# Where the operands of the key, value and query projections lie in SBUF

## The chip, the cores and the metric

The kernel runs on one core of a Trainium2 chip. The metric is the device time of one execution, in microseconds, as the median of several runs.

## The reference, cut to what matters

The program is one inference step of a small encoder with two layers for 512 frames of a new stream and 64 frames of a running one. The 576 rows are treated together; the model width is 1024 and the inner width of the feed-forward network (FFN) 2816. The first layer mixes by a convolution module, the second by stick-breaking attention; each ends with an FFN. Between them the residual stream is normalised and projected once to keys and values:

```python
def rmsnorm(x, g):
    xf = x.astype(jnp.float32)
    y = xf * lax.rsqrt(jnp.mean(xf * xf, axis=-1, keepdims=True) + EPS)
    return (y * g.astype(jnp.float32)).astype(x.dtype)

def swiglu(xn, w_gu, w_down):
    g, u = jnp.split(xn @ w_gu, 2, axis=-1)
    return (jax.nn.silu(g) * u) @ w_down

for l in range(DEPTH):
    ...
    else:
        if l == N_A_LAYERS:
            k_new, v_new = jnp.split(rmsnorm(h, kv_norm_g) @ w_kv, 2, axis=-1)
        ...
        h = h + sb_attention(rmsnorm(h, b_norm_g[j]), k_all, v_all, q_pos, k_pos, w_q[j], w_o[j])
    h = h + swiglu(rmsnorm(h, ffn_norm_g[l]), ffn_w_gu[l], ffn_w_down[l])
```

## The kernel before

The residual stream h lies transposed in SBUF: eight chunks of 128 channels, each 128 partitions by 576 frames. Every matrix product is made of three matmuls on rounded 32-bit halves: an operand is split into a high part (ScalarE: a copy, or a copy scaled by the norm's gain) and a low part (VectorE: the original less the high part), and TensorE multiplies high by high, high by low and low by high, each in two column halves of 288. Weights are split in the same way as they come in, in pieces of 128 x 512: in the later stages a high part goes to a PSUM bank (hp, L522), another to SBUF (wh, L517), and VectorE subtracts (wl, L527).

The FFN's products use a scheme with seven products in place of eight: blocks of weights and of operands are first added or subtracted on GpSimd (S for weights, ta and tb for operands). An operand pair of that scheme is split by `operands` (L1342 high, L1346 low); `product` (L1431) makes the matmuls of one of the seven products on one of a job's three PSUM banks j_A, j_B, j_C; for the down projection VectorE adds each finished product to h (L1664). The down projection runs in three groups of inner channels (0, 1, 2), each over two runs of two jobs: first the output chunks 0, 4, 1 and 5, then 2, 6, 3 and 7. Behind the last group, each finished chunk is squared (ScalarE, L641 and L635) and the squares are added (GpSimd, L644) for the next norm.

The operands x0 to x7 of the key and value projections are h times a gain, split by `split_x` (L740 high, L744 low). The norm's factor r is applied behind the projection: `Norm.rstd` sums the squares over the channels on TensorE (cs_kv, L726), ScalarE and VectorE make r of it (L682 to L703), and the keys (pk, matmuls at L603, evacuated at L1865) are multiplied by it. The values (vk and pv, L1936) have frames on partitions, so r is turned into a column first: five small matmuls (L1845) into a free corner of the tile vk, copied to rc by VectorE (L1848). Then come the queries (pq, L603), with x split anew under another gain, and the attention.

SBUF places. Sixteen places of 128 x 576 named xh0 to xh7 and xl0 to xl7 (pool `xpool`) belong to x0 to x7: high part of chunk c in xhc, low part in xlc. In the FFNs the same sixteen serve, beside 36 others (f) and two double ones (k), as a common store: `single` takes the place at the front of a list, `give` puts a place at its end once the last product that reads its operand is recorded. In the last run of the down projection, the operands of products 2 and 3 of the four channel pairs lie, among others, in xh3, in xh2 and xh4, in xl0 and xl3, and in xl1 and xh5; product 3 is the last one.

Order of the work. Each operation is recorded with its engine, an estimated cost, and what it reads and writes, its places among them. A planner (class `Plan`) then orders everything between two flushes by these costs and dependencies and writes the instructions out in that order, engine by engine; every engine runs its instructions in order. One flush stands at the end of each FFN, so the splits of x0 to x7 for the keys are planned together with the FFN, and the projections together with the attention.

Of the kernel before, what the change touches and what calls it, by code (L numbers as in the profile page):

```python
# [4 lines left out]
F32R = mybir.dt.float32r  # L5
# [5 lines left out]
P = 128  # L11
D = 1024
NC = D // P
SEQ = 512
DEC = 64
T = SEQ + DEC
# [70 lines left out]
ORDER = (0, 4, 1, 5, 2, 6, 3, 7)  # L87
# [25 lines left out]
class Plan:  # L113
# [19 lines left out]
    def op(self, eng, cost, fn, reads=(), writes=(), lat=0.0, group=None, bias=0.0, urgent=False, port=False):  # L133
        i, deps = len(self.ops), set()
        for k in reads:
            if k in self.w:
                deps.add(self.w[k])
            self.r.setdefault(k, []).append(i)
        for k in writes:
            deps.update(self.r.pop(k, ()))  # L140
            if k in self.w:
                deps.add(self.w[k])
            self.w[k] = i
        deps.discard(i)
        self.ops.append((eng, cost, fn, deps, lat, group, bias, urgent, port or eng == "Pool"))
        self.end.append(0.0)
# [75 lines left out]
def build(tc, xT, vec, st, stp, bdp, wt, ck, cv, w_in, w_out, gu, down, wk, wv, wq, wo, yT, csp, css, kp, ks, vp, vs):  # L222
# [6 lines left out]
    xpool = ctx.enter_context(tc.tile_pool(name="xpool", bufs=1))  # L229
# [81 lines left out]
    h = [h_all[:, c, :] for c in range(NC)]  # L311
    X = {}
# [10 lines left out]
    vecs = base.tile([P, NV], F32, name="vecs")  # L323
# [20 lines left out]
    op = plan.op  # L344
# [15 lines left out]
    def act(n, scaled=True):  # L360
        return 0.186 + n * 0.000834 if scaled else 0.16 + n * 0.000715
# [201 lines left out]
    def by_part(tag):  # L563
        return [(tag, 0), (tag, 1)]
# [7 lines left out]
    def H(m):  # L572
        return [("h", m, 0), ("h", m, 1)]
# [144 lines left out]
    def sums_op(key, tag, parts, halves=(0, 1), segs=None, bias=99.0):  # L718

        for j, (t, dep) in enumerate(parts):  # L720
# [9 lines left out]

            op("PE", 4 * len(halves) * pe(HA), f, reads=[dep], writes=tags(tag), bias=bias)

    def split_x(c, g):


        def hi():
            a, b = (xpool.tile([P, T], F32R, name=f"x{p}{c}_{g}", tag=f"x{p}{c}") for p in "hl")
            X[("xt", c)] = (a, b)
            X[("x", c)] = by_half((a, b))
            nc.scalar.activation(a, h[c], AF.Copy, scale=col(g + c))  # L740

        def lo():
            a, b = X[("xt", c)]
            nc.vector.scalar_tensor_tensor(b, h[c], col(g + c), a.bitcast(F32), op0=ALU.mult, op1=ALU.subtract)  # L744

        op("ACT", act(T), hi, reads=H(c) + ["vecs"], writes=[("x", c, "h")] + by_part(f"xh{c}") + by_part(f"xl{c}"))
        op("DVE", dve(T, True), lo, reads=H(c) + [("x", c, "h")], writes=[("x", c, "l")], port=True)

    xkeys = [("x", c) for c in range(NC)]
# [716 lines left out]
    def ffn(l, mixer, g_next, nrm_next, x_busy, k_busy):  # L1466
# [224 lines left out]
        for g in (1, 2):  # L1691
# [10 lines left out]
                            finished(m)  # L1702
            prepare_operands(force=True)
        if g_next is not None:
            for m in ORDER:
                split_x(m, g_next)
        else:
            tail(l, aops[2], nrm_next, finished)
# [391 lines left out]
    def stages(un):  # L2100
# [135 lines left out]
        def stage_v(pi):  # L2236
# [46 lines left out]
            for (j, a, b, o) in jobs:  # L2283

                def hi(j=j, a=a, b=b, o=o):
                    if ("oh", j) not in X:
                        if j < 6:
                            o2 = tile(("ob", j), f"ob{j}" if j < 4 else f"k{j - 4}", (P, KW), F32R, pool=None if j < 4 else kpool)
                            X[("oh", j)], X[("ol", j)] = o2[:, 0:T], o2[:, T:KW]
                        else:  # L2290
                            X[("oh", j)], X[("ol", j)] = (xpool.tile([P, T], F32R, name=f"o{q}{j}", tag=f"x{q}{j}") for q in "hl")
                        X[("o", j)] = by_half((X[("oh", j)], X[("ol", j)]))
                    nc.vector.tensor_copy(X[("oh", j)][:, a:b], oc[:, o : o + b - a])

                def lo(j=j, a=a, b=b, o=o):
                    nc.gpsimd.tensor_tensor(
                        X[("ol", j)][:, a:b], oc[:, o : o + b - a], X[("oh", j)].bitcast(F32)[:, a:b], op=ALU.subtract
                    )

                fk = ("ok", j)  # L2300
                wk, extra = [fk + (a,)], []
                if fk not in X:
                    X[fk] = True
                    wk += oplace(j) + [fk]
                else:
                    extra = [fk]
                op("DVE", 0.08 + (b - a) / 1920, hi, reads=[("oc", 0), ("oc", 1)] + extra, writes=wk, port=True)
                op("Pool", pool(b - a), lo, reads=[("oc", 0), ("oc", 1)], writes=[fk + (a,)])
# [32 lines left out]
    def oproj(i, m, tag):  # L2341
        wi = take()
        k = ("pw", i, m)
        newps(k, tag)

        def deps(xk):
            j = xk[1]
            own = by_part(f"k{j - 4}") if 3 < j < 6 else by_part(f"xh{j}") + by_part(f"xl{j}") if j > 5 else []
            return [("ok", j, 0), ("ok", j, SEQ)] + oplace(j) + own

        mm_ops(k, tag, wi, [("o", j) for j in range(4 * i, 4 * i + 4)], xdeps=deps)
        add_h(m, k, tag)
# [41 lines left out]
    pp = psum_pool("pp3")  # L2394


    ffn(1, lambda i, m: oproj(1, m, (("b0", "b1"), ("b2", "b3"), ("b4", "b5"))[i % 3]), None, Norm("fin"), XT[12:], KT)
    psum.pop().close()
    ctx.close()

# [92 lines left out]
```

## Time and profile before

| | |
|---|---|
| Time, median of 3 runs | 1216.97 us (1216.84 to 1217.43) |
| Profiled execution | 1216.97 us, span 1215.3 us |
| Granted TensorE clock, mean | 0.997 |
| Busy: TensorE, VectorE, ScalarE, GpSimd | 1189.0, 1017.4, 997.6, 805.1 us |
| Down projection of the first FFN ends, keys begin (TensorE) | 588.24 (start of its last matmul), 589.67 us |
| Column sums of the norm for keys and values (cs_kv) | 596.06 us |
| Queries begin | 621.36 us |

In the profile PE is TensorE, PEld its weight loads, DVE VectorE, ACT ScalarE, POOL GpSimd and SP the engine that issues DMAs. "L1431" is a line of the kernel before. A row of a timeline has the start, the duration, the engine, the line, the instruction with output and inputs, how many instructions it merges, and in brackets the idle time of the engine just before it and what ended that. The listed duration of a matmul reaches past the start of the next, since matmuls are pipelined.

### The profile page before, as it was taken

What the parts mean: (1) busy time and instruction counts of PE and PEld (TensorE: products, weight loads), DVE (VectorE), ACT (ScalarE), POOL (GpSimd) and SP (SyncE); (2) the same over time, 40 slices, a digit from 0 to 9 for tenths busy, and PEclk for the clock granted to TensorE, in tenths of its full rate; (3) what the DMA queues carried; (4) which work ended last, traced back from release to release, by engine and by line L of the source; (5) the groups of instructions that cost most, each with busy time, mean ns of one, the idle gap of its engine ahead of it and who ended that gap; (6) DMA issues with size and microseconds to landing.
All of it is one profiled execution on the core that took longest, in us unless ns stands there. A gap on an engine that the chain in (4) does not pass through costs nothing.

```text
span 1215.3 us, 23815 instructions
## 1 busy us (share of the span) xinstructions
PE 1189.0 (98%) x8670; PEld 1160.6 (95%) x8670; DVE 1017.4 (84%) x1643; ACT 997.6 (82%) x1887; POOL 805.1 (66%) x644
## 2 busy tenths in 40 slices
PE   9999989999999999999999999998999999999996
PEld 9999989999999999999998888998999999999996
DVE  7999977978996766998689999979799966668995
ACT  7998474799888888988669999955998989889983
POOL 1999823497867876996204554464698677789951
PEclk9999999999999999999999999999999999999998
DMA  7233822133133323323364333132232323224222
GB/s 275 85 94 94 267 64 84 53 101 109 53 123 107 102 71 104 105 70 106 121 160 104 74 70 72 48 105 70 70 122 70 122 70 122 88 70 124 86 70 78
DMA packets 44997, 121.07 MB, mean 100 GB/s; under 512 B 8784, under 2 KB 14224, under 8 KB 44880
## 3 DMA queue, kind: packets, MB, share of 16 engines
q1 hardware_dynamic: 44448, 118.98, 32.3%
q8 instruction: 68, 1.11, 0.4%
q10 hardware_dynamic: 432, 0.57, 0.1%
q14 instruction: 49, 0.40, 0.1%
HBM read 105.18 MB, written 5.70 MB: 91 GB/s over the span
## 4 chain that ended last, share of the span: by engine, by line
PE 75%; DVE 10%; POOL 2%; ACT 2%; issue 2%; DMA 1%; SPq 0%; DVEq 0%; POOLq 0%; ACTq 0%
PE j_A L1431 31%; PE j_B L1431 16%; PE j_C L1431 8%; PE po L603 4%; PE pw L603 3%; PE b L2225 3%; PE pq L603 3%; DVE acc L1064 2%; PE b L2132 2%; PE av L2252 1%; DVE wl L527 1%; DMA qd<-qd 1%; PE pk L603 1%; PE pd L603 1%; PE pg L603 1%
## 5 line engine op out<-in xcount | busy, mean ns | idle before, releaser
L517 ACT ACTIVATE wh<-wr 128x512 fp32r<-128x512 f32 (+1 forms) x295 | 179.0, 614 | 35.2 <-PE po L603 15.2
L527 DVE TENSOR_TENSOR wl<-S,hp 128x512 fp32r<-128x512 f32 (+1 forms) x258 | 169.5, 663 | 39.9 <-ACT hp L522 36.8
L527 DVE TENSOR_TENSOR wl<-wr,hp 128x512 fp32r<-128x512 f32 (+1 forms) x233 | 154.2, 666 | 43.2 <-ACT hp L522 38.3
L517 ACT ACTIVATE wh<-S 128x512 fp32r<-128x512 f32 (+1 forms) x260 | 155.8, 610 | 8.1 <-PE j_C L1431 3.1
L522 ACT ACTIVATE hp<-S 128x512 fp32r<-128x512 f32 (+1 forms) x258 | 148.8, 581 | 10.7 <-DVE wl L527 5.0
L522 ACT ACTIVATE hp<-wr 128x512 fp32r<-128x512 f32 (+1 forms) x233 | 134.5, 580 | 19.4 <-DVE wl L527 16.0
L447 POOL TENSOR_TENSOR S<-wr,wr 128x512 f32<-128x512 f32 (+1 forms) x65 | 88.3, 1359 | 84.7 <-ACT wh L517 33.5
L1081 POOL TENSOR_TENSOR pacc<-pacc,pr 128x608 f32<-128x608 f32 x69 | 108.9, 1591 | 7.3 <-ACT pr L1078 4.1
L483 POOL TENSOR_TENSOR S<-wr,S 128x512 f32<-128x512 f32 (+1 forms) x65 | 92.6, 1425 | 26.9 <-DVE wl L527 13.7
L447 POOL TENSOR_TENSOR S<-wr 128x512 f32<-128x512 f32 (+1 forms) x65 | 87.5, 1346 | 21.9 <-ACT wh L517 7.6
L447 POOL TENSOR_TENSOR S<-S,wr 128x512 f32<-128x512 f32 (+1 forms) x65 | 91.2, 1403 | 7.6 <-DVE wl L527 6.7
L1608 POOL TENSOR_TENSOR t<-t,r 128x576 f32<-128x576 f32 x44 | 69.2, 1576 | 4.0 <-ACT t L1579 2.8
L1608 POOL TENSOR_TENSOR a<-a,r 128x576 f32<-128x576 f32 x44 | 70.2, 1599 | 1.0 <-DVE a L1585 0.9
L1064 DVE SCALAR_TENSOR_TENSOR acc<-u,vecs,acc 128x608 f32<-128x608 f32 x76 | 64.6, 850 | 1.0
L1078 ACT ACTIVATE pr<-u,vecs 128x608 f32<-128x608 f32 x69 | 54.1, 796 | 8.0 <-POOL pacc L1081 7.7
L1614 DVE TENSOR_TENSOR a<-a,t 128x576 f32<-128x576 f32 x44 | 51.6, 1173 | 6.3 <-ACT t L1612 5.9
L1579 ACT ACTIVATE t<-j_A 128x288 f32<-128x288 f32 x84 | 34.0, 405 | 22.8 <-PE j_A L1431 21.7
L527 DVE TENSOR_TENSOR wl<-wr,wh 128x512 fp32r<-128x512 f32 x62 | 48.9, 800 | 3.7 <-ACT wh L517 3.7
L2225 PE MATMUL b<-s,sums 128*128 128x512 f32 (+1 forms) x196 | 48.4, 357 | 0.0
L1664 DVE TENSOR_TENSOR h<-j_A,h 128x288 f32<-128x288 f32 x92 | 41.2, 449 | 7.5 <-PE j_A L1431 6.8
L1988 POOL COPY qs<-q 128x64 f32<-128x64 f32 x8 | 3.3, 408 | 54.9 <-DVE q L1985 54.9
L1431 PE MATMUL j_A<-('x', 1, 3)_0_b,wh 128*128 128x288 f32 x168 | 35.9, 295 | 0.0
(987 smaller groups left out, 4535.1 us busy)
## 6 DMA issues: line engine op xcount, KB each, us to landing
wr<-gu SPq DMA_DIRECT2D x88, 512.0 KB, 3.6
wr<-down SPq DMA_DIRECT2D x32, 512.0 KB, 3.8
wr<-w_in SPq DMA_DIRECT2D x15, 512.0 KB, 3.8
wm<-wt SPq DMA_DIRECT2D x12, 576.0 KB, 5.6
wr<-down SPq DMA_DIRECT2D x16, 384.0 KB, 3.1
qd<-qd SPq DMA_DIRECT2D x21, 256.0 KB, 2.9
wr<-w_out SPq DMA_DIRECT2D x8, 512.0 KB, 3.7
wr<-wq SPq DMA_DIRECT2D x8, 512.0 KB, 3.5
```

What stands on the lines that cost most here:

```text
L447: eng(e).tensor_tensor(t[:, :n], x[1](), y[1](), op=ALU.subtract if sub else ALU.add)
L483: eng(e).tensor_tensor(v[:, :n], X[("raw", i0)][:, n : 2 * n], v[:, :n], op=ALU.subtract)
L517: nc.scalar.activation(X[("w", u)][0][:, :n], get(), AF.Copy)
L522: nc.scalar.activation(t[:, :n], get(), AF.Copy)
L527: eng(le).tensor_tensor(b[:, :n], get(), a.bitcast(F32)[:, :n], op=ALU.subtract)
L603: nc.tensor.matmul(o[hf], (hi, hi, lo)[j][:, s], (xh, xl, xh)[j], start=(start and q == 0 and j == 0), stop=(stop and q == n - 1 and j == ...
L1064: nc.vector.scalar_tensor_tensor(dst, src, wt_, dst if i else X[("kneg",)], op0=ALU.mult, op1=ALU.add)
L1078: nc.scalar.activation(tile(("pr", c, i), f"pr{m}", (P, YW)), src, AF.Copy, scale=wt)
L1081: nc.gpsimd.tensor_tensor(X[("pacc", c)], X[("pacc", c)], X[("pr", c, i)], op=ALU.add)
L1431: nc.tensor.matmul(out, a[:, s], b, start=(start and q == 0 and i == 0), stop=(q == len(ops_) - 1 and i == 2), skip_group_check=True,)
L1608: nc.gpsimd.tensor_tensor(X[k], X[k], r, op=ALU.mult)
L2225: nc.tensor.matmul(out(zz()), X[(w,)], get(x), start=False, stop=(i == len(mms) - 1), skip_group_check=True)
```

## The change

A table `xmap` says which two places chunk c takes. It starts as before, (xhc, xlc), and the first projections of the program (convolution module) use it so. At the end of the first FFN it is set anew: the list of free x places stands in the order in which the last operands were given back, and the chunks take places from its front, two each, in the order 0, 4, 1, 5, 2, 6, 3, 7, which is the order in which the rows of h are finished. So x0 lies in xl5 and xl4, x4 in xh0 and xl6, x1 in xl2 and xl7, x5 in xh7 and xh1, x2 in xh6 and xh3, x6 in xh2 and xh4, x3 in xl0 and xl3, and x7 in xl1 and xh5. The places that product 3 of the last run still reads then belong to x2, x6, x3 and x7; before, they belonged to x0, x1, x2, x3, x4 and x5. The queries' operands, two chunks of the attention's output (which take the places of x6 and x7) and the second FFN's list of places that are not free yet follow the same table.

```diff
+    xmap = {c: (f"xh{c}", f"xl{c}") for c in range(NC)}
+
     def split_x(c, g):
 
+        tags_ = xmap[c]
 
         def hi():
-            a, b = (xpool.tile([P, T], F32R, name=f"x{p}{c}_{g}", tag=f"x{p}{c}") for p in "hl")
+            a, b = (xpool.tile([P, T], F32R, name=f"x{p}{c}_{g}", tag=t) for p, t in zip("hl", tags_))
...
-        op("ACT", act(T), hi, reads=H(c) + ["vecs"], writes=[("x", c, "h")] + by_part(f"xh{c}") + by_part(f"xl{c}"))
+        op("ACT", act(T), hi, reads=H(c) + ["vecs"], writes=[("x", c, "h")] + by_part(tags_[0]) + by_part(tags_[1]))
...
         if g_next is not None:
+
+            xmap.update({m: tuple(spots["x"][2 * i : 2 * i + 2]) for i, m in enumerate(ORDER)})
             for m in ORDER:
                 split_x(m, g_next)
...
-                            X[("oh", j)], X[("ol", j)] = (xpool.tile([P, T], F32R, name=f"o{q}{j}", tag=f"x{q}{j}") for q in "hl")
+                            X[("oh", j)], X[("ol", j)] = (xpool.tile([P, T], F32R, name=f"o{q}{j}", tag=t) for q, t in zip("hl", xmap[j]))
...
-            own = by_part(f"k{j - 4}") if 3 < j < 6 else by_part(f"xh{j}") + by_part(f"xl{j}") if j > 5 else []
+            own = by_part(f"k{j - 4}") if 3 < j < 6 else by_part(xmap[j][0]) + by_part(xmap[j][1]) if j > 5 else []
...
-    ffn(1, lambda i, m: oproj(1, m, (("b0", "b1"), ("b2", "b3"), ("b4", "b5"))[i % 3]), None, Norm("fin"), XT[12:], KT)
+    ffn(1, lambda i, m: oproj(1, m, (("b0", "b1"), ("b2", "b3"), ("b4", "b5"))[i % 3]), None, Norm("fin"), [t for t in XT if t in xmap[6] + xmap[7]], KT)
```

The planner writes another order for the end of the first FFN (from about 455 us) and for the key and value projections; from the queries on the order is as before on every engine, but for one DMA issue that stands one row earlier. Lines behind the first insertion have numbers that are larger by 3, later by 5 (L740 is L743, L1664 is L1667, L1845 is L1850). Three places:

ScalarE at the end of the down projection, before (xh4 is the high part of x4, sqn a square of a chunk of h, wh0 the first piece of key weights):

```order
L522 ACTIVATE hp_284_7949<-wr92_7733 128x512
L740 ACTIVATE xh7_72_7955<-h_72,vecs_73 128x576
L517 ACTIVATE wh1284_7947<-wr92_7733 128x512
L522 ACTIVATE hp_283_7972<-wr92_7733 128x512
L522 ACTIVATE hp_286_7980<-wr93_7756 128x512
L517 ACTIVATE wh0283_7970<-wr92_7733 128x512
L740 ACTIVATE xh0_72_7988<-h_72,vecs_73 128x576
L740 ACTIVATE xh4_72_7994<-h_72,vecs_73 128x576
L740 ACTIVATE xh1_72_7998<-h_72,vecs_73 128x576
L740 ACTIVATE xh5_72_8002<-h_72,vecs_73 128x576
L740 ACTIVATE xh2_72_8006<-h_72,vecs_73 128x576
L517 ACTIVATE wh3286_7978<-wr93_7756 128x512
```

and with the change:

```order
L641 ACTIVATE sqn_kv_2_3432_7944<-h_72 128x576
L522 ACTIVATE hp_284_7954<-wr92_7753 128x512
L517 ACTIVATE wh1284_7952<-wr92_7753 128x512
L635 ACTIVATE ss_kv_1_7969<-h_72 128x576
L641 ACTIVATE sqn_kv_6_3434_7975<-h_72 128x576
L522 ACTIVATE hp_283_7982<-wr92_7753 128x512
L522 ACTIVATE hp_286_7993<-wr93_7776 128x512
L517 ACTIVATE wh0283_7980<-wr92_7753 128x512
L743 ACTIVATE xh2_72_7998<-h_72,vecs_73 128x576
L743 ACTIVATE xh6_72_8004<-h_72,vecs_73 128x576
L743 ACTIVATE xh3_72_8008<-h_72,vecs_73 128x576
L522 ACTIVATE hp_285_8014<-wr93_7776 128x512
```

The splits of x0, x4, x1 and x5 have gone from here to earlier rows (x4 to 35 rows ahead of the square of h2 with which the piece begins, x0, x5 and x1 to 6 to 11 rows ahead of it); x2, x6 and x3 follow the first key weights, x7 comes three rows after this piece. The square of h7 (ss_kv_1) stands ahead of the key weights; before, it was the last.

TensorE between keys and values, before (the last key matmuls, the column of r, the first value matmuls):

```order
L603 MATMUL pk_1_0_8062<-xh7_72_7955,wl3286_7979 128x288
L603 MATMUL pk_1_1_8063<-xh7_72_7955,wl3286_7979 128x288
L1845 MATMUL vk_8057<-ident_93,r_97 128x1 x5
L1936 MATMUL vk_8057<-wh0287_8146,xh0_72_7988 128x256
L1936 MATMUL vk_8057<-wh0287_8146,xl0_72_7989 128x256
```

and with the change, 24 value matmuls later:

```order
L1941 MATMUL pv_2_8212<-wh1288_8141,xl3_72_8009 128x256
L1941 MATMUL pv_2_8212<-wl1288_8142,xh3_72_8008 128x256
L1850 MATMUL vk_8059<-ident_93,r_97 128x1 x5
L1941 MATMUL pv_3_8259<-wh0287_8114,xh0_72_7828 128x256
L1941 MATMUL pv_3_8259<-wh0287_8114,xl0_72_7829 128x256
```

The column of r stands behind the first two of the five blocks of value matmuls (vk, pv_2), and a block on another tile (pv_3) follows it.

VectorE in group 1 of the down projection, before ("b1" is the operand of product 1, here of group 2; j_26 is the 26th job):

```order
L1346 TENSOR_TENSOR ('a', 0, 2)_1_b1_6686<-a_0_15_5527,('a', 0, 2)_1_b1_6686 128x288
L527 TENSOR_TENSOR wl4240_6928<-S_26_6_6742,hp_240_6929 128x512
L1664 TENSOR_TENSOR h_72<-j_25_A_6669,h_72 128x288
L1614 TENSOR_TENSOR a_0_21_6482<-a_0_21_6482,t1_0_21_6489 128x576
L1664 TENSOR_TENSOR h_72<-j_25_C_6845,h_72 128x288
L1664 TENSOR_TENSOR h_72<-j_26_C_6912,h_72 128x288
L1346 TENSOR_TENSOR ('a', 0, 2)_2_b1_6698<-a_0_16_5777,('a', 0, 2)_2_b1_6698 128x288
L527 TENSOR_TENSOR wl5241_6972<-S_27_7_6917,hp_241_6973 128x512
L1664 TENSOR_TENSOR h_72<-j_25_A_6669,h_72 128x288
L527 TENSOR_TENSOR wl0242_6984<-S_28_7_6956,hp_242_6985 128x512
L1346 TENSOR_TENSOR ('a', 0, 2)_3_b1_6950<-a_0_17_5844,('a', 0, 2)_3_b1_6950 128x288
L1664 TENSOR_TENSOR h_72<-j_26_A_6755,h_72 128x288
```

and with the change:

```order
L1349 TENSOR_TENSOR ('a', 0, 2)_0_b1_6661<-a_0_14_5459,('a', 0, 2)_0_b1_6661 128x288
L527 TENSOR_TENSOR wl4240_6931<-S_26_6_6750,hp_240_6932 128x512
L1667 TENSOR_TENSOR h_72<-j_25_A_6672,h_72 128x288
L1617 TENSOR_TENSOR a_0_21_6473<-a_0_21_6473,t1_0_21_6489 128x576
L1667 TENSOR_TENSOR h_72<-j_25_C_6847,h_72 128x288
L527 TENSOR_TENSOR wl5241_6968<-S_27_7_6895,hp_241_6969 128x512
L1667 TENSOR_TENSOR h_72<-j_25_A_6672,h_72 128x288
L1667 TENSOR_TENSOR h_72<-j_26_C_6915,h_72 128x288
L1617 TENSOR_TENSOR a_0_20_6452<-a_0_20_6452,t1_0_20_6432 128x576
L527 TENSOR_TENSOR wl1243_6988<-wr80_6790,hp_243_6989 128x512
L1667 TENSOR_TENSOR h_72<-j_26_A_6760,h_72 128x288
```

Of the four product-1 operands of group 2 (pairs 0 to 3), all are split up to here before, and one with the change; the other three follow later.

## The prediction

> **What bounds the kernel now.** I read the page first, then the busy time by stage, then who waited for whom on TensorE around the change, and last the timelines of single engines there.
>
> ```profile
> PE 1189.0 (98%) x8670; PEld 1160.6 (95%) x8670; DVE 1017.4 (84%) x1643; ACT 997.6 (82%) x1887; POOL 805.1 (66%) x644
> PE 75%; DVE 10%; POOL 2%; ACT 2%; issue 2%; DMA 1%; SPq 0%; DVEq 0%; POOLq 0%; ACTq 0%
> ```
>
> TensorE is busy 98% of the span and three quarters of the chain that ended last are its own work. So only time in which TensorE stands still can be won, and anything that makes it stand still is lost. The stages that the change touches are the end of the first FFN's down projection and the key and value projections:
>
> ```profile
> core 0: us, PE busy (x) PEld busy (x) DVE busy (x) ACT busy (x) POOL busy (x), PEclk, DMA share, GB/s
> 500.00:520.00 20.00, 19.63 (x147) 19.19 (x146) 19.70 (x32) 17.87 (x33) 18.11 (x14) 1.00 0.33 106
> 520.00:540.00 20.00, 19.47 (x147) 19.24 (x146) 19.13 (x33) 17.98 (x34) 20.00 (x17) 1.00 0.34 106
> 540.00:560.00 20.00, 20.00 (x151) 19.83 (x150) 19.38 (x33) 16.05 (x30) 13.31 (x12) 1.00 0.31 85
> 560.00:580.00 20.00, 20.00 (x153) 20.00 (x152) 14.53 (x28) 18.12 (x33) 12.31 (x10) 1.00 0.32 102
> 580.00:600.00 20.00, 18.54 (x131) 17.58 (x130) 13.62 (x22) 14.61 (x26) 6.24 (x8) 1.00 0.35 116
> ```
>
> The columns that matter are PE, DVE, ACT and POOL busy out of 20 us. The granted clock is 1.00 throughout. From 500 to 560 DVE has hardly a gap (19.70, 19.13, 19.38); from 560 on DVE and ACT have room. TensorE's largest loss is in the last stretch. Its waits from 400 to 640 us, by cause (total, times, longest):
>
> ```profile
> PE pk L603 <- ACT xh L740: 1.1, 1, 1.1
> PE j_A L1431 <- DVE h L1664: 0.8, 2, 0.5
> PE pk L603 <- DVE xl L744: 0.3, 1, 0.3
> PE vk L1936 <- DVE rc L1848: 0.3, 1, 0.3
> ```
>
> They sum to 2.5 us, so nothing here can be worth many microseconds. The list counts only idle time; a matmul's listed end reaches past the start of its successor, so I take the loss from the distance of starts. The first row below is a piece of the chain of waits (start, duration, matmuls), the others are TensorE's timeline (start, duration, instruction, count, idle time before it and what ended it):
>
> ```profile
> 598.16 7.18 PE pk L603 x54
> 588.24 0.29 PE L1431 MATMUL j_A<-('a', 0, 2)_3_b,wl 128*128 128x288 f32 x1
> 589.67 0.53 PE L603 MATMUL pk<-xh,wh 128*128 128x288 f32 x2 [1.14 <-ACT xh L740]
> 590.53 0.53 PE L603 MATMUL pk<-xl,wh 128*128 128x288 f32 x2 [0.32 <-DVE xl L744]
> 596.06 2.10 PE L726 MATMUL cs_kv_None<-ss_kv,ones 128*128 128x288 f32 x8
> ```
>
> Undisturbed, 54 matmuls of 288 columns take 7.18 us, 0.133 each. The last matmul of the down projection starts at 588.24, so the first key matmul (pk) could start at 588.37. It starts at 589.67, when the high part of x0 is there (1.30 lost), and the low part of x0 holds the third matmul until 590.53, against 589.94 (0.59 lost). Up to the norm's column sums (cs_kv) at 596.06 stand 42 key matmuls: 42 x 0.133 = 5.59, which from 588.37 ends at 593.96. **Lost at this boundary: 596.06 - 593.96 = 2.10 us.**
>
> **The change, part by part.** It adds and removes no instruction. Each operand chunk x0 to x7 gets two places in SBUF, and only the assignment changes; the order written by the planner follows from it.
>
> (1) *The boundary.* Before, places held to the last product belong to six of the eight chunks, x0 to x5; now they belong to x2, x3, x6 and x7, whose h rows are finished last anyway. The splits of x0, x4, x1 and x5 go ahead of the last three products. What is the last wait now? The timeline of ScalarE, and last a row of VectorE's:
>
> ```profile
> 582.71 0.69 ACT L641 ACTIVATE sqn_kv<-h 128x576 f32<-128x576 f32 x1 [2.93 <-DVE h L1664]
> 585.00 0.69 ACT L641 ACTIVATE sqn_kv<-h 128x576 f32<-128x576 f32 x1 [0.57 <-POOL ss_kv L644]
> 585.59 0.58 ACT L522 ACTIVATE hp<-wr 128x512 fp32r<-128x512 f32 x1
> 588.34 0.61 ACT L517 ACTIVATE wh<-wr 128x512 fp32r<-128x512 f32 x1
> 588.86 3.43 ACT L740 ACTIVATE xh<-h,vecs 128x576 fp32r<-128x576 f32 x5
> 589.66 3.73 DVE L744 SCALAR_TENSOR_TENSOR xl<-h,vecs,xh 128x576 fp32r<-128x576 f32 x5
> ```
>
> Start to start, a square (sqn) takes 0.59, a bank copy (hp) and a weight split (wh) 0.52 each, an x split 0.67 (3.43 for five); five low parts on VectorE take 3.73, 0.75 each. The key projection needs wh of its first weights, which ended at 588.95 before, and it now becomes the late one. The square of h2 opens the row. It started at 582.71, on h2's last update. In the new order the last three matmuls of that product stand behind the next product of twelve, so it comes 12 x 0.133 = 1.6 us later, at 584.3. Behind it stand in the new order square, hp, wh, square, square, hp, hp and then the wh: 3 x 0.59 + 4 x 0.52 = 3.85, so the wh starts at 588.15, with 0.05 more for Pool's addition in front of the third square (a wait that was 0.57), and ends at 588.8. TensorE starts at 588.9 instead of 589.67, and its first 24 matmuls (x0, x4, x1, x5; 3.2 us) find both parts ready. Then x2, x6, x3 follow the wh on ScalarE from 588.7; x7 comes after them, one hp and two wh: 588.7 + 3 x 0.67 + 3 x 0.52 = 592.3, its low part by 593.9. TensorE wants it 42 matmuls after 588.9, at 594.5: 0.6 to spare. The column sums now follow 54 key matmuls, at 588.9 + 7.18 = 596.1, and need the last square (593.0 to 593.7) and Pool's addition:
>
> ```profile
> 593.99 1.43 POOL L644 TENSOR_TENSOR ss_kv<-ss_kv,sqn_kv 128x576 f32<-128x576 f32 x1 [4.71 <-ACT sqn_kv L641]
> ```
>
> 593.7 + 0.1 + 1.43 = 595.2, so 0.9 to spare. Loss at the boundary now: 588.9 - 588.37 = 0.53. **Gain 2.10 - 0.53 = 1.57.** Bounds: 0.59 if the wh only ends when x0 did before (589.6), 2.10 if h2's square is not late.
>
> (2) *The column of r for the values.* TensorE waits there for a copy on VectorE (two rows of TensorE's timeline, one of VectorE's, two pieces of the chain of waits):
>
> ```profile
> 607.61 0.28 PE L1936 MATMUL vk<-wl,xh 128*128 128x256 f32 x1
> 608.15 0.39 PE L1936 MATMUL vk<-wh,xh 128*128 128x256 f32 x1 [0.26 <-DVE rc L1848]
> 607.93 0.17 DVE L1848 COPY rc<-vk 128x5 f32<-128x5 f32 x1 [2.26 <-PE vk L1936]
> 609.84 4.32 PE pv L1936 x36
> 621.36 12.00 PE pq L603 x90
> ```
>
> Value matmuls go at 4.32 / 36 = 0.12. After 607.61 the next could start at 607.73; it starts at 608.15: 0.42 lost. The copy waited 2.26 us, until the twelve value matmuls on the same PSUM tile (vk) had passed, though what it reads was written before them. In the new order these twelve and twelve more stand ahead of the r columns, and twelve on another tile behind them (1.44 us), so the copy is done under those. **Gain 0.42**, bounds 0 (the copy is late behind the k rows, which VectorE now takes first) and 0.42. r itself comes later, since the new order puts two weight splits ahead of its last step on VectorE (2 x 0.68 by a row below), but 24 x 0.12 = 2.9 us of value matmuls now stand ahead of its reader. From here the value matmuls and the first queries (pq) run without a gap in the chain, and the order after them is unchanged on every engine, so I take the gain to reach the end whole.
>
> (3) *The down projection itself.* The planner also wrote another order back to about 455 us. What it can win is bounded by TensorE's two large stalls there, and what it can lose by VectorE (rows of both timelines):
>
> ```profile
> 506.81 0.29 PE L1431 MATMUL j_B<-('a', 0, 1)_3_b,wl 128*128 128x288 f32 x1
> 507.41 0.51 PE L1431 MATMUL j_A<-('a', 0, 1)_0_b,wh 128*128 128x288 f32 x2 [0.31 <-DVE h L1664]
> 520.39 0.29 PE L1431 MATMUL j_B<-('a', 0, 1)_3_b,wl 128*128 128x288 f32 x1
> 521.22 0.54 PE L1431 MATMUL j_A<-('a', 0, 1)_0_b,wh 128*128 128x288 f32 x2 [0.53 <-DVE h L1664]
> 501.71 0.45 DVE L1346 TENSOR_TENSOR ('a', 0, 2)_0_b<-a,('a', 0, 2)_0_b 128x288 fp32r<-128x288 f32 x1
> 512.70 1.26 DVE L1346 TENSOR_TENSOR ('a', 0, 2)_1_b<-a,('a', 0, 2)_1_b 128x288 fp32r<-128x288 f32 x1
> 516.85 1.58 DVE L1346 TENSOR_TENSOR ('a', 0, 2)_2_b<-a,('a', 0, 2)_2_b 128x288 fp32r<-128x288 f32 x1
> 518.36 0.68 DVE L527 TENSOR_TENSOR wl<-S,hp 128x512 fp32r<-128x512 f32 x1
> 519.91 0.88 DVE L1346 TENSOR_TENSOR ('a', 0, 2)_3_b<-a,('a', 0, 2)_3_b 128x288 fp32r<-128x288 f32 x1
> ```
>
> 507.41 - 506.81 - 0.133 = 0.47 and 521.22 - 520.39 - 0.133 = 0.70: 1.17 in all, both released by an update of h on VectorE, which came late behind operand and weight splits. In the new order three of the four group-2 low halves shown (1.26, 1.58, 0.88) and three weight splits (0.68) fewer stand ahead of the twelfth h update. That work is not gone: it lies behind, between 520 and 560. Upper bound 1.17; lower bound below. **I take half, 0.6.** The extra ScalarE work before 588 costs nothing: four x splits, 4 x 0.67 = 2.7 us, where ScalarE idled 2.93 us in one piece (row 582.71). On SP one load of query weights moves up by one row; nothing waits for it there.
>
> Sum: 1.57 + 0.42 + 0.6 = 2.6 us. The profiled execution took 1216.97 us (1.67 around its span), the same as the median shown, so I forecast **1214.4 us**.
>
> **Rivals.**
>
> *A: the weights take the place of the operands.* If ScalarE reaches the wh of the first weights only when x0 was ready before, TensorE starts at 589.67 as it did, and only x0's low part (0.59) and the column copy (0.42) are won: 1216.97 - 1.0 = 1216.0. For it: ScalarE does everything in order, and in front of this wh stand three squares, each with a wait (h2, h7, Pool). Against it: the walk above has 0.8 us left.
>
> *B: everything goes.* h2's square is not late, the wh is early, and both stalls of the down projection vanish: 2.10 + 0.42 + 1.17 = 3.7, so 1213.3. For it: at the second stall the new order puts another product of nine matmuls (1.2 us) in front of the one that waited.
>
> *C: slower; VectorE falls behind from 520 to 560.* There it idles 0.87 + 0.62 = 1.49 us. The work moved in is 1.26 + 1.58 + 0.88 + 3 x 0.68 = 5.76 by the rows. If TensorE has to wait for all that does not fit, it loses 4.27, less the 1.99 of (1) and (2): 1216.97 + 2.3 = 1219.3. It decides from the point where the overflow exceeds 2 us. For it: POOL is busy 20.00 of 20 us from 520 to 540, and the same low half took 0.45 us in one place and 1.58 in another. The Trainium skill, page "SBUF — State Buffer", section "Who interferes with whom", says that a VectorE instruction with two SBUF inputs contends with a GpSimd instruction that reads SBUF; these low halves are such instructions, and the trace agrees (0.45 against 1.58). By that rule the moved halves stay long in the new place. Against it: VectorE idles over 5 us from 560 to 580, so an overflow drains there unless a product needs it sooner.
>
> *D: no effect.* The splits stay where h lets them be; 1217.0. The changed order speaks against it.
>
> **How the numbers follow.** Forecast 0.45, A 0.26, B 0.22, C 0.05, D 0.02. A measurement of this kernel tells about 0.2% (2.43 us, below 1214.54) from no change. B and a little more than half of the forecast's spread (0.28) lie beyond it: faster 0.50. A, D and the rest of the forecast's (0.17) lie within: same 0.45. Slower 0.05. The range runs from a little below B, 1212.8, to a little above A, 1216.6; the forecast's own is 1213.6 to 1215.2.
>
> **What would show it.** In the changed profile: the first key matmul starts within 0.7 us of the down projection's last, with a ScalarE weight split and no x split as its releaser, and no wait for a low part follows; the wait for the column copy is gone; the stretch from 500 to 540 shows less than the 0.84 us of TensorE idle that two of its waits have now, and 540 to 560 none over 0.3. Wrong would be: a wait of the key matmuls for x2 or x7, of the column sums for Pool, or of down products for group-2 operands of more than 1 us; or an x split that still stands as releaser of the first key matmul.

## The result and the profile after

The changed kernel takes 1219.70 us (median of 14 runs, 1218.6 to 1220.34); the kernel before took 1217.23 on the same chip (14 runs). The ratio is 1.0019, 95% interval 1.0012 to 1.0026: **2.5 us slower**, where 2.6 us less was forecast. The profiled execution took 1219.54 us, its span is 1217.8.

Up to the attention's last product the change does what was forecast. TensorE's waits from 400 to 640 us and its timeline at the boundary, and a row of ScalarE's timeline:

```profile
PE j_A L1434 <- DVE h L1667: 0.7, 2, 0.4
PE pk L603 <- ACT wh L517: 0.4, 1, 0.4
```

```profile
588.19 0.29 PE L1434 MATMUL j_A<-('a', 0, 2)_3_b,wl 128*128 128x288 f32 x1
588.86 0.55 PE L603 MATMUL pk<-xh,wh 128*128 128x288 f32 x2 [0.37 <-ACT wh L517]
596.17 2.11 PE L726 MATMUL cs_kv_None<-ss_kv,ones 128*128 128x288 f32 x8
588.19 0.61 ACT L517 ACTIVATE wh<-wr 128x512 fp32r<-128x512 f32 x1
```

The first key matmul starts 0.67 us behind the last down product (before: 1.43) and waits for a weight split, no x split. No wait for a low part or for the column of r is left. The 54 key matmuls end with the column sums at 596.17, so 588.19 + 0.133 + 7.18 = 595.50 leaves 0.67 lost (before: 2.10). What makes the kernel slower stands 200 us later. TensorE at the end of the attention, before, and then with the change (av is the attention's output, ob, oh and ol operands of the output projection, pw its products):

```profile
795.00 0.78 PE L2252 MATMUL av<-e,vv 128*128 128x512 f32 x2
795.62 0.99 PE L603 MATMUL pw<-ob,wh 128*128 128x288 f32 x4
800.85 0.53 PE L603 MATMUL pw<-oh,wh 128*128 128x288 f32 x2
802.57 0.54 PE L603 MATMUL pw<-ol,wh 128*128 128x288 f32 x2 [1.19 <-POOL ol L2296]
```

```profile
793.00 0.63 PE L2257 MATMUL av<-e,vv 128*128 128x512 f32 x2
798.31 0.85 PE L603 MATMUL pw<-ob,wh 128*128 128x288 f32 x4 [4.69 <-DVE oc L2283]
799.44 1.16 PE L603 MATMUL pw<-ob,wh 128*128 128x288 f32 x4
802.30 0.69 PE L603 MATMUL pw<-ob,wh 128*128 128x288 f32 x4
```

The last attention product starts at 793.00 instead of 795.00: 2.00 won so far. Two matmuls of 0.24 later the output projection of the second half of the heads could begin, at 793.48. It begins at 798.31: **4.83 us lost in one wait**, for the row oc on VectorE, the last step of copying av out of PSUM (its evacuation). Before, the same product began at 795.62, 0.14 after it could. Behind the wait the matmuls are slow: 18 of them take 3.99 us from 798.31 to 802.30 instead of 18 x 0.133 = 2.39, another **1.60**. In return the waits of 0.30 (at 795.62 to 796.45, before) and 1.46 (800.85 to 802.57) are gone, since those operands are ready by now. -2.00 + 4.83 - 0.14 + 1.60 - 1.76 = +2.53 at this place; the spans differ by 2.5.

What the wait hangs on (one row each of GpSimd, ScalarE and VectorE), and the stretches by granted clock (TensorE's busy time in 2 us, PEclk):

```profile
794.70 0.76 POOL L2301 TENSOR_TENSOR ol<-oc,oh 128x64 fp32r<-128x64 f32 x1
795.49 1.20 ACT L2280 ACTIVATE oc<-av 64x512 f32<-64x512 f32 x2 [1.93 <-POOL ol L2301]
796.77 1.39 DVE L2283 TENSOR_TENSOR oc<-av,oc 64x512 f32<-64x512 f32 x2 [1.49 <-issue]
```

```profile
core 0: us, PE busy (x), PEclk, DMA share, GB/s
794.00:796.00 2.00, 0.00 (x0) 1.00 0.47 131
798.00:800.00 2.00, 1.69 (x9) 0.71 0.09 30
800.00:802.00 2.00, 2.00 (x10) 0.50 0.84 225
802.00:804.00 2.00, 2.00 (x16) 0.93 0.09 37
```

ScalarE's copy of av (oc) waits for GpSimd, which still reads the tile oc of the pair before; VectorE's addition follows, ends at 798.16, and 0.15 later TensorE goes on. The granted clock then stands at 0.71 and 0.50 and comes back by 804.

**Why the same product did not wait before.** The order on TensorE is the same there; what it waits for is not. The program's own rows, before and with the change:

```
4804 L603 MATMUL pw_4_0_10573<-ob_10031,wh_10350 128x288 [waits DVE_49]
4805 L603 MATMUL pw_4_1_10574<-ob_10031,wh_10350 128x288 [waits DVE_49]

4804 L603 MATMUL pw_4_0_10573<-ob_10031,wh_10350 128x288 [waits DVE_49,PE_49,Activation_49]
4805 L603 MATMUL pw_4_1_10574<-ob_10031,wh_10350 128x288
```

The reason is the PSUM bank. A PSUM pool of this kernel gives a tag its banks when the first tile of that tag is made, and the tile is made where the planner puts the matmul that opens it (`newps`, an operation without cost). The re-planned order makes the column sums of the norm (cs_kv) before the tiles of values and keys. From the addresses in the two programs:

| banks | before | with the change | next pool, in both |
|---|---|---|---|
| 0, 1 | vk, last used as av | cs_kv, last used as scores b4, b5 | cs_f |
| 2, 3 | pk_0, last used as pw_7 | vk, last used as **av** | **pw_4**, the first product |
| 4, 5 | cs_kv, last used as b4, b5 | pk_0, last used as pw_7 | pw_0 |
| 6, 7 | pk_1, last used as b2, b3 | pk_1, last used as b2, b3 | pw_1 |

The next pool opens at the end of the attention. Its first product lies in banks 2 and 3 in both kernels; before, these held pw_7, which VectorE had read, and now they hold av, the last thing that the attention leaves.

### The profile page after: what moved, and what is told of

The parts are those of the page before. It is cut to its first block, busy times and chain, and to the rows that moved or that the text cites. A ratio compares the mean times of both kernels' runs of the same rounds, so it can differ in the third digit from the quotient of the medians.

```text
span 1217.8 us, 23814 instructions
## 1 busy us (share of the span) xinstructions
PE 1189.6 (98%) x8670; PEld 1161.7 (95%) x8670; DVE 1021.1 (84%) x1643; ACT 997.7 (82%) x1887; POOL 808.6 (66%) x644
## 4 chain that ended last, share of the span: by engine, by line
PE 74%; DVE 9%; ACT 2%; issue 2%; DMA 2%; POOL 1%; SPq 0%; DVEq 0%; POOLq 0%; ACTq 0%
PE j_A L1434 30%; PE j_B L1434 15%; PE j_C L1434 7%; PE po L603 4%; PE pw L603 4%; PE b L2230 3%; PE pq L603 3%; PE b L2137 2%; DVE wl L527 1%; DVE acc L1067 1%; PE av L2257 1%; DMA qd<-qd 1%; PE pk L603 1%; PE pd L603 1%; PE pg L603 1%
## 5 line engine op out<-in xcount | busy, mean ns | idle before, releaser
L1667 DVE TENSOR_TENSOR h<-j_A,h 128x288 f32<-128x288 f32 x92 | 41.4, 450 | 4.4 <-PE j_A L1434 3.8
L603 PE MATMUL pw<-ob,wh 128*128 128x288 f32 x192 | 34.5, 303 | 4.7 <-DVE oc L2283 4.7
```

The lines of the kernel that those rows point to most:

```text
L603: nc.tensor.matmul(o[hf], (hi, hi, lo)[j][:, s], (xh, xl, xh)[j], start=(start and q == 0 and j == 0), stop=(stop and q == n - 1 and j == ...
```

## The experiments

Starts on TensorE in the profiles (us), and medians. Each ratio is against runs of the kernel before on the same chip, whose median was 1217.44 us beside e1 to e4, 1217.65 beside e5 to e8 and 1217.63 beside e9 and e10:

| kernel | last down product | first key matmul | first product pw_4 | first gate matmul | median | ratio, interval |
|---|---|---|---|---|---|---|
| before | 588.24 | 589.67 | 795.62 | 824.91 | 1217.23 | |
| change | 588.19 | 588.86 | 798.31 | 827.20 | 1219.70 | 1.0019 (1.0012, 1.0026) |
| e1 banks of before | 586.52 | 587.19 | 792.08 | 821.37 | 1214.24 | 0.9975 (0.9965, 0.9984) |
| e2 banks of change | 586.78 | 588.21 | 798.95 | 828.91 | 1222.10 | 1.0037 (1.0024, 1.0049) |
| e3 matmuls in the wait | 586.61 | 587.28 | 796.28 | 823.59 | 1216.11 | 0.9992 (0.9983, 1.0001) |
| e4 own oc | 586.47 | 587.13 | 792.04 | 820.08 | 1212.59 | 0.9962 (0.9949, 0.9974) |
| e5 change again | 586.70 | 587.36 | 797.00 | 826.23 | 1219.84 | 1.0018 (1.0009, 1.0027) |
| e6 before again | 588.30 | 589.73 | 795.86 | 825.14 | 1217.29 | one run |
| e7 light VectorE | 586.45 | 586.85 | 791.79 | 821.08 | 1213.70 | 0.9972 (0.9960, 0.9983) |
| e8 places reversed | 588.31 | 590.39 | 797.17 | 826.45 | 1218.63 | 1.0006 (0.9997, 1.0014) |
| e9 best banks, own oc | 586.98 | 587.64 | 792.50 | 820.39 | 1212.93 | 0.9962 (0.9948, 0.9975) |
| e10 change, own oc | 586.39 | 587.06 | 795.13 | 823.91 | 1217.25 | 0.9996 (0.9987, 1.0004) |

### Order and banks, one at a time (e1, e2)

To the changed kernel e1 adds tiles that are made once, in a fixed order, right after the pool is opened:

```diff
     pp = psum_pool("pp2")
+    for i, (tag, n) in enumerate([('v', 2), ('b0', 1), ('b1', 1), ('b4', 1), ('b5', 1), ('b2', 1), ('b3', 1)]):
+        tile(("first", i), tag, (P, 512 * n), pool=pp)
```

> The changed kernel with one addition: right after the PSUM pool of the attention part is opened, its tiles are created once in the order of the kernel before (v, b0, b1, b4, b5, b2, b3), so that each name gets the PSUM banks that it has in the kernel before. The order of instructions on every engine is that of the changed kernel. Theory P (the loss is the PSUM banks: the re-planned order created the column sums' tiles first, so the first output product of the second FFN's section inherits the banks of the attention's last tile av): the 4.83 us wait at 793 us goes, the slow matmuls behind it too, the small waits of the kernel before come back (0.30 and 1.46), and the gain up to 640 us stays: 1217.2 - 2.0 = 1215.2. Rival S (the loss is the SBUF places: the attention's outputs o6 and o7 or the second FFN's free places moved with the table): the wait stays, 1219.7. Rival N (any re-planning moves the end by some us either way): no prediction, but 1215.2 within 0.3 would be a coincidence.

To the kernel before, e2 adds the same lines with the order b4, b5, v, b0, b1, b2, b3.

> The kernel before, whose order stays, with the tiles of the same pool created once in the order of the changed kernel (b4, b5, v, b0, b1, b2, b3). Theory P: the same wait appears at about 795 us without any change of the operands' places: 4.83 us of wait and 1.6 us of slower matmuls behind it, less the 0.30 and 1.46 that the kernel before loses there: 1217.2 + 4.5 = 1221.7. Rival S: 1217.2, no wait there.

Both leave the order of every engine as it was; only waits of a few matmuls differ. TensorE's timelines, e1 and then e2:

```profile
791.46 0.78 PE L2259 MATMUL av<-e,vv 128*128 128x512 f32 x2
792.08 0.99 PE L603 MATMUL pw<-ob,wh 128*128 128x288 f32 x4
797.30 0.53 PE L603 MATMUL pw<-oh,wh 128*128 128x288 f32 x2
799.02 0.53 PE L603 MATMUL pw<-ol,wh 128*128 128x288 f32 x2 [1.18 <-POOL ol L2303]
```

```profile
793.51 0.78 PE L2254 MATMUL av<-e,vv 128*128 128x512 f32 x2
798.95 1.30 PE L603 MATMUL pw<-ob,wh 128*128 128x288 f32 x4 [4.66 <-DVE oc L2280]
```

With the banks of before the wait is gone, and e1 takes 1214.24: 3.2 us less than the kernel before and 5.5 less than the changed one. With the banks of the change, the kernel before gets the wait (4.96 lost, with no edit to places or order) and takes 1222.1, 4.7 us more. Theory P said 1215.2 and 1221.7. S (places in SBUF) is out, and so is N (any re-planning), since nothing is re-planned in e2 and the wait is there. e1 is a microsecond better than P said; its profile reaches the last down product 1.67 earlier than the first one of the change (more on that below).

### What the wait is made of (e10, e3)

e10 is the changed kernel, banks included, in which the last pair's oc lies in a place of x0 that is free by then:

```diff
+            own = {0: oc}
+            if un.i == len(pairs) - 1:
+                own.clear()
+            def place_oc():
+                if not own:
+                    own[0] = xpool.tile([P, T], F32, name="oc2", tag=xmap[0][0])
+                return own[0]
...
-                    return two(oc[m, :w])
+                    return two(place_oc()[m, :w])
```

(the two operations behind it read `place_oc()` likewise).

> The changed kernel with its own banks, and the own place for the last pair's oc as in e4_own_oc: nothing but the evacuation of av gets earlier. Theory P (the first output product waits until VectorE has read av): ScalarE's copy of av need not wait for GpSimd, VectorE's addition then starts behind its two weight splits, 1.5 us earlier, and the wait of 4.83 us falls to about 3.4; 1219.7 - 1.5 = 1218.2 if the clock still falls to one half behind it, 1216.6 if it does not. Rival W (it waits for the weights, which ScalarE splits behind the copy): the wait stays over 4.5, 1219.5.

Rows of TensorE, ScalarE and VectorE in e10:

```profile
791.27 0.78 PE L2257 MATMUL av<-e,vv 128*128 128x512 f32 x2
795.13 1.30 PE L603 MATMUL pw<-ob,wh 128*128 128x288 f32 x4 [3.09 <-DVE oc L2290]
792.08 1.20 ACT L2287 ACTIVATE oc<-av 64x512 f32<-64x512 f32 x2 [0.25 <-PE av L2257]
793.61 1.38 DVE L2290 TENSOR_TENSOR oc<-av,oc 64x512 f32<-64x512 f32 x2
```

The copy now follows av by 0.25 us, VectorE's addition ends at 794.99, and TensorE goes on at 795.13: lost 795.13 - 791.27 - 0.48 = 3.38, as said. The wait is the evacuation of av. The clock falls again, so of the two cases it is that of 1218.2; the median of 1217.25 is 0.95 better. The span is 2.2 us shorter than e5's: 1.6 is the wait, and about 0.45 the slow clock behind it (28.78 against 29.23 us from the first product to the first gate matmul).

e3 lets TensorE work through the wait of the changed kernel:

```diff
     flush()
+    hold = pp.tile([P, 512], F32, name="hold", tag="b2")
+    for i in range(18):
+        nc.tensor.matmul(hold, X[("oner",)], vv[0], start=True, stop=True)
     section()
     att_pool.close()
```

> The changed kernel with 18 matmuls of 512 columns on a free PSUM bank behind the last attention product, so that TensorE works through most of the 4.83 us wait (18 x 0.24 = 4.3 us) and nothing else moves. Theory C (part of the loss is that TensorE runs slower after a long wait: the granted clock is 0.97 and 0.94 in the two stretches around it, and the 18 matmuls after it take 1.6 us more than 18 x 0.133): the wait's end stays where it is, the matmuls behind it run at 0.133 each, 1219.7 - 1.6 = 1218.1, and the granted clock stays 1.00. Rival L (they are slow because weights or operands come late): 1219.7, still slow.

TensorE's timeline and its clock by stretches in e3, then the clock in e5, the changed kernel once more:

```profile
792.17 4.27 PE L2399 MATMUL hold<-vv,sums 128*128 128x512 f32 x18
796.28 0.69 PE L603 MATMUL pw<-ob,wh 128*128 128x288 f32 x4
```

```profile
796.00:798.00 2.00, 2.00 (x16) 1.00 0.04 9
```

```profile
796.00:798.00 2.00, 1.00 (x4) 0.50 0.40 145
798.00:800.00 2.00, 2.00 (x10) 0.50 0.48 76
800.00:802.00 2.00, 2.00 (x13) 0.71 0.49 195
```

With work in it the clock stays at 1.00 and four matmuls take 0.53 us again; in e5 the clock is at 0.50 from 796 to 800, while four matmuls take 0.96 (798.58 to 799.54). From the first product to the first gate matmul the changed kernel takes 28.89 and 29.23 us in its two profiles, e3 27.31: the slow clock costs 1.6 and 1.9, where theory C of e3 said 1.6. e3 is faster than the 1218.1 of this theory. In its profile the time from the last attention product on is shorter too (796.28 - 791.56 - 0.48 = 4.24 us against 4.96 in e5): the edit also moved two squares on ScalarE behind the added matmuls, GpSimd reached the last read of oc earlier, and VectorE had finished by 795.1. That part was not meant.

### The places themselves (e8)

On top of e1, the table is turned round:

```diff
-            xmap.update({m: tuple(spots["x"][2 * i : 2 * i + 2]) for i, m in enumerate(ORDER)})
+            xmap.update({m: tuple(spots["x"][14 - 2 * i : 16 - 2 * i]) for i, m in enumerate(ORDER)})
```

> As e1_banks_of_before, with the table of places turned round: the places that are held to the last product go to x0, x4, x1 and x5, which the key projection wants first, and the free ones to the others. Theory (first term of the prediction: what counts is that the first chunks' places are free before the last product): the splits of x0 stand behind the last down product again, the first key matmul comes about 1.3 us behind it and the low part holds the third by 0.6, so the boundary loses about 2.1 as in the kernel before, instead of 0.54: e1_banks_of_before + 1.5 = 1215.7, and 0.4 more if the column of r waits again. Rival N (any re-planning with the same banks does it): 1214.2.

TensorE's timeline at the boundary, and a stretch by clock:

```profile
588.31 0.29 PE L1434 MATMUL j_A<-('a', 0, 2)_3_b,wl 128*128 128x288 f32 x1
590.39 0.53 PE L603 MATMUL pk<-xh,wh 128*128 128x288 f32 x2 [1.78 <-ACT xh L743]
591.24 0.62 PE L603 MATMUL pk<-xl,wh 128*128 128x288 f32 x2 [0.32 <-DVE xl L747]
592.14 0.68 PE L603 MATMUL pk<-xh,wh 128*128 128x288 f32 x2
```

```profile
592.00:594.00 2.00, 2.00 (x10) 0.50 0.98 398
```

The two waits are back, for the x split and its low part, 1.95 and 0.59 us, and here they too halve the clock: from 591.66 to 594.54 twelve matmuls take 2.88 us instead of 1.60. 1218.63 is 4.4 us above e1 (5.0 by the spans), where 1.5 was expected. N is out: with the same banks, which chunk gets which places decides between a gain of 3.2 us and none. The size was missed by the clock (1.3), a first wait longer by 0.65 than in the kernel before, and 1.8 us in the down projection of this profile. The last need not be chance: the planner's order for the reversed table is close to that of the kernel before (in the two programs, 63 of TensorE's matmuls stand elsewhere than there, 420 elsewhere than in the change), and the stalls of the kernel before are back with it (0.42 at 519 us, 0.69 at 521).

### The down projection (e5, e6, e7)

e5 and e6 are the changed kernel and the one before, unchanged, for second profiles. e7 is e1 with each update of h in the first FFN's down projection on 32 columns instead of 288, so it leaves out most of what this projection adds to h.

> The changed kernel once more, unchanged, for a second profile on the chip of the next three. Question: its first profile has three stalls of TensorE in the down projection (0.52, 0.53 and 0.24 us, released by updates of h on VectorE) and reaches the last down product at 588.19; the runs with the banks of before, whose order is the same there, have none of them and reach it at 586.52. Theory J (VectorE has no slack from 500 to 560, and whether its stalls reach TensorE falls out anew in each execution): the profile shows either picture, and the times lie in groups about 1.5 us apart. Rival B (the bank placement itself acts back on the down projection): the three stalls are there again, and 588.2.

> The kernel before once more, for a second profile. First profile: stalls of 0.47 and 0.70 and smaller ones, last down product at 588.24; the run with the banks of the change and the order of before has one of 0.47 and reaches it at 586.78. Theory J: either picture, times in groups about 1.5 us apart (1216 and 1217.4). Rival B: 588.2 again.

> As e1_banks_of_before, and each update of h in the first FFN's down projection takes 32 columns instead of 288 (most of what that down projection adds is left out), at the same place of VectorE's order and at the same planned cost, so that the order of all engines stays. That takes some 0.27 us off each of the about 45 updates from 500 to 560, so VectorE has over 10 us of slack there. Theory J (the third term of the prediction is VectorE's slack): no stall over 0.2 us from 455 to 586, the last down product at 586.5 or a little before, and the times in one group near the faster one of e1_banks_of_before, 1213.8 within 0.4. Rival D (the spread of the times comes from the transfers of the first 200 us or from the end): the times of e1_banks_of_before with both groups, median 1214.2.

Rows of TensorE in the first profile of the change, in its second, and in the second of the kernel before:

```profile
537.57 0.51 PE L1434 MATMUL j_A<-('a', 0, 1)_0_b,wh 128*128 128x288 f32 x2 [0.35 <-DVE h L1667]
546.54 0.50 PE L1434 MATMUL j_A<-('a', 0, 2)_0_b,wh 128*128 128x288 f32 x2 [0.37 <-DVE h L1667]
```

```profile
586.70 0.29 PE L1434 MATMUL j_A<-('a', 0, 2)_3_b,wl 128*128 128x288 f32 x1
```

```profile
521.28 0.53 PE L1431 MATMUL j_A<-('a', 0, 1)_0_b,wh 128*128 128x288 f32 x2 [0.53 <-DVE h L1664]
588.30 0.29 PE L1431 MATMUL j_A<-('a', 0, 2)_3_b,wl 128*128 128x288 f32 x1
```

In its first profile the change has traded the stalls at 507 and 521 for others at 537, 546 and 566 (0.52, 0.53, 0.24). In its second they are all but gone, and the last down product comes at 586.70, as in e1, e3, e4, e9 and e10, which have the same order up to there. The order before reaches it at 588.24, 588.30 and, in e2, 586.78. So rival B is out, and **the same program reaches this product some 1.5 us earlier or later from execution to execution**: late in one of seven profiles of the new order, in two of three of the old, which is too few to speak of odds. A part of it comes before this stage. The last matmul up to which both orders agree starts at 444.38 and 444.83 in the two profiles of the kernel before, and at 444.77 and 444.49 in those of the change. From there to the last down product it takes 143.86 and 143.47 before, 143.42 and 142.21 with the change. In e7 no stall of over 0.2 us is left there, the last product comes at 586.45, and 4 of 6 runs take 1213.5 to 1213.7; two are at 1214.7 and 1215.5, so VectorE's slack is not all of the spread; what the rest is stays open. The busy time of the engines there, change and e7 (the third figure behind 20.00 is VectorE's, 20.00 and 14.74):

```profile
540.00:560.00 20.00, 19.63 (x148) 19.42 (x147) 20.00 (x35) 15.95 (x29) 9.77 (x8) 1.00 0.29 84
540.00:560.00 20.00, 20.00 (x153) 20.00 (x153) 14.74 (x32) 15.94 (x30) 11.06 (x10) 1.00 0.32 107
```

### Beyond the change (e4, e9)

e4 is e1 with the own place for oc of e10.

> As e1_banks_of_before, and the last pair's output column tile oc lies in a place of x0, which is free by then, so that ScalarE's copy of av need not wait until GpSimd has read the tile of the pair before (idle 2.08 us before it in the kernel before, released by the low part on GpSimd). Theory: the copy starts about 2 us earlier, VectorE's addition 1.5 us earlier, the low part of the last output operand ends at about 800.8 on the clock of the kernel before instead of 802.5, and TensorE's 1.46 us loss there goes: 1215.2 - 1.4 = 1213.8. Rival: another wait is right behind it (the weights of the next product, ScalarE's weight splits) and half or more comes back: 1214.5 to 1215.2.

In e4 the wait of 1.46 for the last low part is down to 0.33:

```profile
797.73 0.54 PE L603 MATMUL pw<-ol,wh 128*128 128x288 f32 x2 [0.17 <-POOL ol L2310]
```

1212.59 us, 4.9 less than the kernel before; where 1.4 less than e1 was expected, 1.65 came. e9 gives the first product the banks that are free earliest:

> As e4_own_oc (the changed kernel with the banks given by hand, and an own place for the last pair's oc), but the banks are given in the order v, b4, b5, b0, b1, b2, b3: the first output product of the second FFN's section gets the banks of the attention's scores (b4, b5), which are free earliest, and the second one those of the product before (b0, b1). Theory P: the 0.30 us that TensorE loses at the first output product in e4_own_oc goes, nothing else moves: 1212.6 - 0.3 = 1212.3. Rival: the low part of the last output operand is waited for by 0.3 more: 1212.6.

```profile
792.50 0.69 PE L603 MATMUL pw<-ob,wh 128*128 128x288 f32 x4
798.20 0.53 PE L603 MATMUL pw<-ol,wh 128*128 128x288 f32 x2 [0.47 <-POOL ol L2310]
```

The loss of 0.30 behind the first product is gone, and the wait for the low part has grown from 0.33 to 0.64: the rival was right, 1212.93 is not better. What bounds here is the chain from av to that low part.

## Why the prediction was wrong, point by point

**The step that failed** is the last sentence of part (2): the order behind the values is unchanged on every engine, "so I take the gain to reach the end whole". An unchanged order does not mean unchanged waits. The new order ahead of it made the tiles of the attention's pool in another sequence, so the banks changed, and the first product behind the attention inherited av's. e1 and e2 show it from both sides: by the medians the banks alone cost 4.7 us on the old order and 5.5 on the new. No rival had this. C came closest in number (1219.3) by a mechanism that did not occur.

**What bounds the kernel**: right. What moved in these profiles was TensorE's waits and its clock behind them, not its work; but what was read as "nothing here can be worth many microseconds" holds for a gain from waits that are there, and says nothing of a wait that is not there yet.

**(1) The boundary**: right. First key matmul forecast at 588.9, measured 588.86, its releaser the weight split; no wait for x2 or x7; column sums forecast at 596.1, measured 596.17. Gain forecast 1.57, measured 2.10 - 0.67 = 1.43. e8 shows that it hangs on the order of the places.

**(2) The column of r**: right. 0.42 was forecast, 0.49 came: from the column sums to the first query matmul it takes 25.14 us before (596.06 to 621.20; the 621.36 given ahead is a row of the chain of waits) and 23.05 with the change (596.17 to 619.22). 1.60 of the 2.09 are the twelve key matmuls that now stand ahead of the sums. VectorE's copy no longer holds TensorE:

```profile
607.79 0.16 DVE L1853 COPY rc<-vk 128x5 f32<-128x5 f32 x1 [0.74 <-PE vk L1850]
```

**(3) The down projection**: right in kind, wrong as one number. 0.6 was half of the stalls of one profile. From 444 us on the stage takes 143.4 to 143.9 us or 141.8 to 142.5 in these profiles; in the first pair the change gains 0.44 there, in the second 1.26. That it makes the short time more frequent is not shown by so few. By the medians e1 wins 3.2, so (1) and (2) leave about 1.3 for it, a little over the upper bound of 1.17.

**The sum**: with the banks held, 1214.24 was measured where 1214.4 was forecast. That they lie so close is in part luck: 3.2 us were won where 2.6 were forecast, and the kernel before took 1217.44 beside e1, not the 1216.97 that the forecast started from.

**Rival C** priced the three moved low halves at the durations they had, and took from the rule on contention (the Trainium skill, "SBUF — State Buffer", "Who interferes with whom") that they would stay long. In the new place they took half of that:

```profile
521.27 0.57 DVE L1349 TENSOR_TENSOR ('a', 0, 2)_1_b<-a,('a', 0, 2)_1_b 128x288 fp32r<-128x288 f32 x1
537.71 0.80 DVE L1349 TENSOR_TENSOR ('a', 0, 2)_2_b<-a,('a', 0, 2)_2_b 128x288 fp32r<-128x288 f32 x1
542.43 0.55 DVE L1349 TENSOR_TENSOR ('a', 0, 2)_3_b<-a,('a', 0, 2)_3_b 128x288 fp32r<-128x288 f32 x1
```

0.57, 0.80 and 0.55 instead of 1.26, 1.58 and 0.88. What differs is how much was left of the instruction that GpSimd was running when the low half began. Two rows of GpSimd, the one under the low half of 1.58 before and the one under that of 0.57 with the change:

```profile
516.82 1.30 POOL L447 TENSOR_TENSOR S<-S,wr 128x512 f32<-128x512 f32 x1
520.71 0.81 POOL L1377 TENSOR_TENSOR ('a', 0, 2)_0_tb<-a,('a', 0, 2)_0_tb 128x288 f32<-128x288 f32 x1
```

The first ends at 518.12 and its low half at 518.43, the second at 521.52 and its low half at 521.84; all six end 0.31 to 0.33 us behind such an instruction. So they do contend with GpSimd, as that rule has it; that a moved one stays long does not follow.

**A, B, D**: A's condition did not occur (0.8 us of room forecast, the split came in time); B and D are out by the first key matmul.

## What to carry to other kernels

When an edit lets a planner reorder work, compare the two programs by what each instruction waits for and by the addresses of its tiles, not by the order alone; the changed wait of row 4804 was there to be read before any run. Where pools give out places by first use, fix the sequence by hand, so that an edit in one stage cannot hand a late tile's bank to the first matmul of another. Price a wait of TensorE of some 2 us or more at its length and the slow clock behind it, here 1.3 to 2.65 us.

## What the runs showed of the hardware

A long wait of TensorE is paid twice. In these traces the granted clock then goes to 0.50 for 3.4 us or for twice that: from 798.86 to 802.27 in the change, 794.89 to 798.30 in e10, 794.32 to 801.15 in e5 and 797.89 to 804.71 in e2. In the change it falls only 0.55 us after TensorE has gone on, in e5 2.7 us before. What it costs follows from how much of this time TensorE has work, 3.4, 3.2, 4.15 and 5.8 us; a little less than half of that is lost: 1.6, 1.5 (28.78 us from the first product to the first gate matmul, against 27.31 in e3), 1.9 and 2.65 (29.96). So waits of nearly the same length, 4.83 in the change and 4.96 in e5 and e2, cost 1.6 to 2.65 us behind them. In e8 two waits of 1.95 and 0.59 with two matmuls between them sufficed (0.50 from 591.54 to 594.95), while the 1.30 and 0.59 of the kernel before left it at 1.00. The Trainium skill ("TensorE: Matmul & The Clock Gate", Part 1) has half the clock after an idle window of about 3.4 us and the full one after as much work; these runs agree on the half and on the step of 3.4 us, but e8 lost the clock without a window that was idle throughout.
